# Seven sweeps of block products for the out-projection of a decoder block

## The chip, the cores and the metric

The kernel runs on one core of a Trainium2 chip. The metric is device microseconds of one execution. TensorE multiplies, VectorE and ScalarE work on what it needs and leaves, GpSimd does small copies, and SyncE issues every transfer between the memory of the core and that of the chip.

## The reference

One layer of a decoder on 2,048 tokens with 1,024 features, in float32. `D_LRU` is 1024, `D_SC` 512, `D_FF` 3072.

```python
h = rms_norm(x, norm1_g[l])
z = jnp.einsum('bsd,de->bse', h, w_in[l])               # 1024 -> 3584
lru_x, lru_gate, sc_b, sc_c, sc_x = jnp.split(z, splits, axis=-1)
lru_x = causal_dwconv(lru_x, lru_conv_w[l]) + lru_conv_b[l]
y_lru = rg_lru(lru_x, ...) * jax.nn.gelu(lru_gate)
y_sc = sc_b * causal_dwconv(sc_c * sc_x, sc_conv_w[l])
y_mix = jnp.concatenate([y_lru, y_sc], axis=-1)         # 1536
x = x + jnp.einsum('bse,ed->bsd', y_mix, w_out[l])      # the out-projection
h = rms_norm(x, norm2_g[l])
u = causal_dwconv(jnp.einsum('bsd,df->bsf', h, w_up[l]), ffn_conv_w[l])
gate, up = jnp.split(u, 2, axis=-1)
x = x + jnp.einsum('bsf,fd->bsd', jax.nn.gelu(gate) * up, w_down[l])
...
return rms_norm(x, final_g)
```

## The kernel before

Everything is held with features on the 128 partitions and tokens along the row. The tokens are worked in two halves of 1,024, each of two blocks of 512. The stages follow each other on TensorE: in-projection, recurrence and short convolution of half 0 (here called in0), out-projection of half 0 (out0), in1, out1, then up- and down-projection of both halves (up0, down0, up1, down1).

Each product is made of three matmuls in a rounded format: an operand is split into a rounded part `hi` (a ScalarE copy) and the rest `lo` (a VectorE subtraction) by `split`, and `hi·hi`, `hi·lo` and `lo·hi` are added up in PSUM.

*The order.* TensorE and SyncE run in the order in which the program text issues their instructions. The other engines' instructions are ordered by a planner, by the place in the text, brought forward by `high_priority`: 120 places for whatever empties PSUM, 90 for splits of weights. SyncE issues transfers one after the other, and a transfer whose tile or data isn't ready holds up all behind it.

*The in-projection.* `in_phase` goes through 12 units in the order `UNITS` (L0 L1 S0 L2 L3 S1 L4 L5 S2 L6 L7 S3). A unit of kind L is 128 features of the recurrence (two input products, two gate products, a scan), a unit of kind S 128 features of the short convolution (three input products). `load_weights` loads 512 KB of weights for one product, splits them and calls `tick`. A unit's result `y` (128 × 1,024) is written to the chip's memory by `defer(4, ...)`: four `tick`s later, which is after the fourth weight load behind it. `tick` sends what is due from the head of a list, in order, so an entry that isn't due holds back those behind it. After units 3 to 8 `between` calls `down_sums`, which loads four blocks of `w_down`, makes four sums (S1 to S4) and writes them out, with `defer(3, ...)`.

*The out-projection.* `project` takes a block of 512 tokens at a time and fills eight PSUM banks, one for each 128 of the 1,024 output features. It goes through the 12 rows of 128 features of `y` two at a time: `load_k2` loads 1 MB of `w_out` and two blocks of 256 KB of `y` and splits them. At the end of a block the residual (x) is added from PSUM and the sum is stored, its squares added to an accumulator. During out0 `x1_beside` loads and splits x of half 1, during out1 `h_beside` calls `h_prep` four times, which makes h of half 0 and its combinations for the up-projection.

*The down-projection.* `sweeps` treats its product as 2 × 2 blocks: output features in two halves, input features in pairs of 128, tokens in two blocks. Seven products of sums of blocks take the place of eight products of blocks. `SWEEPS` names the weight block and the data block of each sweep, `TAKEN` the output blocks to which a sweep's PSUM is added (or from which it is subtracted). Four banks `x` run through sweeps 0, 2, 4 and 6 without being cleared; sweeps 1, 3 and 5 have four banks `y` of their own. A step is one load of 512 KB of weights and 512 KB of data, two splits of each and 24 matmuls. The data are written by `up_rest`: blocks B11, B21, B22 and the combinations T1 to T4.

*Buffers.* Raw loads have two tiles (`wr`), split operands 10 pages of 4 KB (`w`), long-lived pages 28 (`act`), short-lived ones 7 (`tmp`); the sums of squares, their splits and roots, `down_sums` and `sq` live in `tmp`.

Of the kernel before, what the change touches and what calls it, by code (L numbers as in the profile page):

```python
# [7 lines left out]
F32 = mybir.dt.float32  # L8
# [20 lines left out]
NI = NFF // 2  # L29
W_OPS = ["W21", "W11", "W22", "W12"]  # L30
# [34 lines left out]
def block_kernel(  # L65
# [34 lines left out]
    y_d = [[dr.tile([P, T], F32, name=f"y_d{h}_{k}") for k in range(NOUT)] for h in range(NH)]  # L100
    f_d = [{o: [dr.tile([P, 2, NB], F32, name=f"f_d{h}_{o}_{k}") for k in range(NI // 2)] for o in F_OPS} for h in range(NH)]
    s_d = {o: [dr.tile([P, 2, NB], F32, name=f"s_d{o}_{k}") for k in range(NI // 2)] for o in S_OPS}
# [72 lines left out]
    def tick():  # L175
        for w in waiting:
            w[0] -= 1
        while waiting and waiting[0][0] <= 0:
            _, dst, src = waiting.pop(0)
            nc.sync.dma_start(dst, src)  # L180
# [209 lines left out]
    def in_phase(half, acts, acc, between):  # L390
# [27 lines left out]
        for n, (kind, c) in enumerate(UNITS):  # L418
# [22 lines left out]
            defer(4, y_d[half][n], y)  # L441
# [4 lines left out]
    def load_k2(src, spilled, t, k, name, ypage):  # L446
        raw = raw_tile(f"wr_{name}_{k}")
        w = raw[:, 0:4, :].rearrange("p (k a) c -> p k (a c)", k=2)
        nc.sync.dma_start(w, src[k : k + 2].rearrange("k p m -> p k m"))
        for i in range(2):  # L450
            nc.sync.dma_start(raw[:, 4 + i, :], spilled[k + i][:, blk(t)])
        tick()
        out = []
        for i in range(2):
            hi = flat(wpage(f"wh_{name}_{k + i}"))
            lo = flat(wpage(f"wl_{name}_{k + i}"))
            yb = ypage(f"yb_{name}_{k + i}")
            with tc.high_priority(offset=HW):
                split(yb[:, 0, :], yb[:, 1, :], raw[:, 4 + i, :])
                split(hi, lo, w[:, i, :])  # L460
            out.append(((hi, lo), yb))
        return out

    def project(half, nk, src, spilled, name, residual, done, beside, late=None, last_k=0):
        step = 0
        for t in range(T // NB):
            pss = [pst(f"{name}{half}_{t}_{i}") for i in range(KC)]
            fin = last_k if t == T // NB - 1 else 0
            held = []
            res = None  # L470

            def steps(k, wt, yb, ms):
                for m in ms:
                    mm3(pss[m], wcol(wt, m), (yb[:, 0, :], yb[:, 1, :]), k == 0, k == nk - 1)

            wts = None
            for k in range(nk):
                if k % 2 == 0:
                    wts = load_k2(src, spilled, t, k, f"{name}{half}_{t}", act if last_k else wpage)
                wt, yb = wts[k % 2]  # L480
                if k == nk - 4:
                    res = [residual(t, i) for i in range(KC // 2)]
                if t > 0 and late is not None and k < 3:
                    if k == 2:
                        late()
                    steps(k, wt, yb, range(KC - 1))
                    held.append((k, wt, yb))
                    if k == 2:
                        for h in held:
                            steps(*h, (KC - 1,))  # L490
                        held = []
                elif k >= nk - fin:
                    held.append((k, wt, yb))
                else:
                    steps(k, wt, yb, range(KC))
                beside(step)
                step += 1
            for i in range(KC // 2):
                for m in (2 * i, 2 * i + 1) if held else ():
                    for h in held:  # L500
                        steps(*h, (m,))
                    with tc.high_priority(offset=HP):
                        nc.vector.tensor_tensor(res[i][:, m % 2, :], pss[m], res[i][:, m % 2, :], ALU.add)
                    done(t, i, res[i], m % 2)
                if not held:
                    with tc.high_priority(offset=HP):
                        for m in range(2):
                            nc.vector.tensor_tensor(res[i][:, m, :], pss[2 * i + m], res[i][:, m, :], ALU.add)
                    done(t, i, res[i], None)
# [14 lines left out]
    def x_residual(half):  # L524
        def get(t, i):
            r = res_page(f"xr{half}_{t}_{i}", i % 2)
            o = half * T + t * NB
            nc.sync.dma_start(r, xT[2 * i : 2 * i + 2, :, o : o + NB].rearrange("m p c -> p m c"))
            return r

        return get

    def x2_residual(half, alloc):
        def get(t, i):
            r = alloc(f"x2r{half}_{t}_{i}")
            nc.sync.dma_start(r, x2_d[half][i][:, :, blk(t)].rearrange("m p c -> p m c"))
            return r

        return get
# [124 lines left out]
    def up_rest(half, j, ug, un):  # L664
        cg, cu = flat(tmp(f"cg{half}_{j}")), flat(tmp(f"cu{half}_{j}"))
        conv(cu, un, 3, O_FCW + 3 * (NFF + j))
        conv(cg, ug, 3, O_FCW + 3 * j)
        nc.scalar.activation(cg, cg, AF.Gelu_apprx_tanh)
        nc.vector.scalar_tensor_tensor(cu, cg, -1.0, cu, ALU.mult, ALU.mult)
        when = {NFF - 2: 3, NFF - 1: 6}.get(j, 1)  # L670
        i = j // 2

        def put(op, src):
            defer(when, f_d[half][op][i // 2][:, i % 2, :], src)

        t0, t1 = blk(0), blk(1)
        if j % 2 == 0:
            put("B11", cu[:, t0])
            even.append(cu)
            return  # L680
        a, b, c, d = even.pop(), cu, cg, flat(tmp(f"tt{half}_{j}"))
        put("B21", b[:, t0])
        put("B22", b[:, t1])
        nc.vector.tensor_tensor(c[:, t0], a[:, t0], a[:, t1], ALU.subtract)
        nc.vector.tensor_tensor(d[:, t0], b[:, t1], a[:, t1], ALU.subtract)
        nc.vector.scalar_tensor_tensor(c[:, t1], c[:, t0], -1.0, b[:, t1], ALU.mult, ALU.subtract)
        nc.vector.scalar_tensor_tensor(d[:, t1], c[:, t1], -1.0, b[:, t0], ALU.mult, ALU.subtract)
        put("T1", c[:, t0])
        put("T2", c[:, t1])
        put("T3", d[:, t0])  # L690
        put("T4", d[:, t1])
# [25 lines left out]
    def down_sums(i):  # L717
        a, b, c = tmp(f"sa{i}"), tmp(f"sb{i}"), tmp(f"sc{i}")
        for o, dst in zip(W_OPS, (a[:, 0, :], a[:, 1, :], b[:, 0, :], b[:, 1, :])):
            nc.sync.dma_start(dst, w_down[W_OPS.index(o), i // 2].rearrange("p (k c) -> p k c", k=2)[:, i % 2, :])  # L720
# [5 lines left out]
        for o, src in zip(S_OPS, (c[:, 0, :], c[:, 1, :], a[:, 0, :], b[:, 1, :])):  # L726
            defer(3, s_d[o][i // 2][:, i % 2, :], src)

    def sums_at(first, i0, also=None):
        def between(n):  # L730
            if also is not None:
                also(n)
            if first <= n < first + NI // 2:
                down_sums(i0 + n - first)

        return between
# [73 lines left out]
    in_phase(0, None, ss1[0], sums_at(3, 0))  # L810
# [5 lines left out]
    def x1_beside(s):  # L816
        if s in (4, 5, 6, 7, 16, 17, 18, 19):
# [4 lines left out]
    def out_done(half):  # L822
        def done(t, i, r, part):
            store_pair(x2_d[half][i], t, r)
            add_squares(ss2[half], t, i, r, f"b{half}")

        return done

    project(0, NOUT, w_out, y_d[0], "o", x_residual(0), out_done(0), x1_beside)
# [13 lines left out]

    in_phase(1, x1, ss1[1], sums_at(3, NI // 2, late_mean(ss2[0], "b0", rs2[0], 1)))

# [10 lines left out]
    project(1, NOUT, w_out, y_d[1], "o", x_residual(1), out_done(1), h_beside(0, (3, 6, 16, 18)))  # L856
# [5 lines left out]
    def down_w(o, i2):  # L862
        if o in W_OPS:
            return w_down[W_OPS.index(o), i2].rearrange("p (k c) -> p k c", k=2)
        return s_d[o][i2]
# [10 lines left out]
    def down0_done(key, m, r):  # L876
        if m % 2 == 0:
            return
        mh, t = PLACE[key]
        store_pair(x3_d[2 * mh + m // 2], t, r, 2 if key == "21" else 4)  # L880
        add_squares(ss3, t, 0 if key in ("11", "22") and m == 1 else 1, r, f"c0{key}{m}")

# [7 lines left out]
        down0_done,  # L890
# [68 lines left out]

def _arrange(i):  # L960
# [8 lines left out]
    for g, name in enumerate(("lru_wa", "lru_wx")):  # L969
# [5 lines left out]
    out["w_out"] = w[[c if kind == "L" else NLRU + c for kind, c in UNITS]]  # L975
    w = f["w_down"][0].reshape(NI // 2, 2, 2, P, 2, NB)
    out["w_down"] = np.stack(
        [w[:, :, kh, :, mh].transpose(0, 2, 1, 3).reshape(NI // 2, P, T) for mh, kh in ((1, 0), (0, 0), (1, 1), (0, 1))]
    )
# [40 lines left out]
```

## Time and profile before

| | |
|---|---|
| median of 3 runs | 2334.21 us (2332.16 to 2335.15) |
| the profiled execution | 2334.49 us |
| its span | 2332.7 us |
| in0 | 0 to 344.1 us |
| out0 | 344.1 to 476.2 us |
| in1 | 476.2 to 804.4 us |
| out1 | 804.4 to 937.1 us |
| up0, down0 | to 1395 and to 1623.5 us |
| up1, down1 and the end | to about 2079 and to 2332.7 us |

In the lines below, PE is TensorE's matmuls and PEld its weight loads, DVE is VectorE, ACT ScalarE, POOL GpSimd, SP SyncE; L189 is line 189 of the kernel. A line of the chain has the start, the duration, and what ran or was waited for; a line of the timeline the start, the duration, the engine and the instruction. In a table by stage each engine has its busy time and, in brackets, its instructions; then come the granted clock, the busy share of the transfer engines and GB/s. In a line of a group the two numbers after the first bar are busy microseconds and mean nanoseconds of one; after the second bar stands the idle time ahead of them.

### The profile page before, as it was taken

Reading aid. Unit: us, or ns where it says so; the run is one execution under the profiler, and the core shown is the slowest. Engines: PE = TensorE matmul, PEld = TensorE weight load, DVE = VectorE, ACT = ScalarE, POOL = GpSimd, SP = SyncE. Lnnn points to the kernel's source line nnn. Section 1 sums busy time; section 2 is a strip of 40 time slices with the busy share of each in tenths; the row PEclk is TensorE's granted clock in tenths of the full one; section 3 lists DMA queues with packets and bytes.
Section 4 is the critical chain, followed back from the end, with each engine's and each line's share of the span. In section 5 each row is a group of like instructions: output and inputs, shape, how many; then the busy total and the mean of one; then the engine's idle time right before and its main releaser. Section 6 shows DMA issues by size and latency. Waiting matters only on the chain.

```text
span 2332.7 us, 26351 instructions
## 1 busy us (share of the span) xinstructions
PE 2306.0 (99%) x10128; PEld 1903.2 (82%) x10128; DVE 1693.3 (73%) x1890; ACT 1125.5 (48%) x1254; POOL 135.7 (6%) x194
## 2 busy tenths in 40 slices
PE   8999999999999999999999999999999999999997
PEld 7888888888888887888888888888888888887885
DVE  7766665666666777888787877678788787886556
ACT  5553454445543644554444444445544444443343
POOL 0000000000000000011111110000011111100000
PEclk9999999999999999999999999999999999999998
DMA  4134335632334366332333337576223232348654
GB/s 151 68 120 138 138 130 189 251 104 68 133 125 158 116 221 223 117 114 99 111 107 109 105 135 280 198 252 235 86 91 113 91 113 93 117 173 318 244 189 180
DMA packets 141183, 349.99 MB, mean 150 GB/s; under 512 B 13056, under 2 KB 16256, under 8 KB 141056
## 3 DMA queue, kind: packets, MB, share of 16 engines
q1 hardware_dynamic: 141056, 348.30, 42.6%
q8 instruction: 79, 1.29, 0.2%
q14 instruction: 48, 0.39, 0.1%
HBM read 258.07 MB, written 90.18 MB: 149 GB/s over the span
## 4 chain that ended last, share of the span: by engine, by line
PE 95%; DVE 3%; DMA 1%; ACT 1%; issue 0%; SPq 0%; DVEq 0%; ACTq 0%
PE zin_b L222 26%; PE zx L608 22%; PE zc L608 11%; PE o L189 11%; PE dx L754 9%; PE dy L754 8%; PE za L608 6%; PE zi_b L222 1%; PE zr_b L222 1%; DMA wr_d<-s_dS 0%; DVE x2r L791 0%; DVE x2r L898 0%; DMA wr_o<-y_d 0%; DMA fx<-x_d 0%; DVE fl_d L184 0%
## 5 line engine op out<-in xcount | busy, mean ns | idle before, releaser
L222 PE MATMUL zin_b<-xh,wh_in 128*128 128x512 f32 x896 | 277.9, 391 | 5.3 <-DVE ss_a L258 2.6
L222 PE MATMUL zin_b<-xl,wh_in 128*128 128x512 f32 x896 | 277.1, 390 | 0.3 <-DVE xl L380 0.3
L222 PE MATMUL zin_b<-xh,wl_in 128*128 128x512 f32 x896 | 276.9, 390 | 0.0
L189 PE MATMUL o<-yb_o,wh_o 128*128 128x512 f32 x768 | 236.8, 389 | 1.3 <-ACT wh_o L183 1.3
L222 PEld LDWEIGHTS zin_b<-xh,wh_in 128*128 128x128 f32 x896 | 169.0, 189 | 41.7 <-DVE ss_a L258 3.5
L222 PEld LDWEIGHTS zin_b<-xl,wh_in 128*128 128x128 f32 x896 | 168.7, 189 | 36.6 <-DVE xl L380 1.8
L222 PEld LDWEIGHTS zin_b<-xh,wl_in 128*128 128x128 f32 x896 | 168.7, 188 | 35.2
L184 DVE TENSOR_TENSOR fl_d<-wr_d,fh_d 128x1024 fp32r<-128x1024 f32 x84 | 102.8, 1223 | 101.2 <-ACT fh_d L183 99.1
L183 ACT ACTIVATE fh_d<-wr_d 128x1024 fp32r<-128x1024 f32 x84 | 89.0, 1060 | 177.7 <-PE dy L754 79.7
L189 PEld LDWEIGHTS o<-yb_o,wh_o 128*128 128x128 f32 x768 | 144.0, 188 | 31.9 <-ACT wh_o L183 2.1
L184 DVE TENSOR_TENSOR wla_up<-wr_up,wha_up 128x1024 fp32r<-128x1024 f32 x48 | 58.8, 1226 | 140.4 <-ACT wha_up L183 140.4
L754 PE MATMUL dx<-fl_d,wh_d 128*128 128x512 f32 x384 | 149.6, 390 | 1.3 <-DVE fl_d L184 1.3
L189 PE MATMUL o<-yb_o,wl_o 128*128 128x512 f32 x384 | 149.7, 390 | 1.1 <-DVE wl_o L184 1.1
L183 ACT ACTIVATE wh_in<-wr_in 128x1024 fp32r<-128x1024 f32 (+1 forms) x62 | 60.2, 975 | 186.3 <-DMA wr_in<-in_w_in 174.7
L754 PE MATMUL dx<-fh_d,wh_d 128*128 128x512 f32 x384 | 149.4, 389 | 0.0
L754 PE MATMUL dx<-fh_d,wl_d 128*128 128x512 f32 x384 | 149.4, 389 | 0.0
L584 DVE TENSOR_TENSOR wr_up<-wr_up 128x512 f32<-128x512 f32 x192 | 130.2, 686 | 9.2 <-DMA wr_up<-in_w_up 7.6
L184 DVE TENSOR_TENSOR wl_d<-wr_d,wh_d 128x1024 fp32r<-128x1024 f32 x84 | 102.6, 1221 | 40.8 <-ACT wh_d L183 38.3
L184 DVE TENSOR_TENSOR wl_in<-wr_in,wh_in 128x1024 fp32r<-128x1024 f32 (+1 forms) x62 | 69.1, 1118 | 83.4 <-ACT wh_in L183 75.3
L608 PE MATMUL zc<-hhB,whd_up 128*128 128x512 f32 x384 | 126.0, 389 | 0.0
L282 DVE SCALAR_TENSOR_TENSOR cu<-un,prm,cu 128x1024 f32<-128x1024 f32 x96 | 122.7, 1278 | 4.3 <-ACT cu L278 4.3
L282 DVE SCALAR_TENSOR_TENSOR cg<-ug,prm,cg 128x1024 f32<-128x1024 f32 x96 | 122.9, 1280 | 0.7
(238 smaller groups left out, 5289.4 us busy)
## 6 DMA issues: line engine op xcount, KB each, us to landing
wr_up<-in_w_up SPq DMA_DIRECT2D x96, 512.0 KB, 4.8
wr_in<-in_w_in SPq DMA_DIRECT2D x54, 512.0 KB, 4.2
wr_o<-in_w_out SPq DMA_DIRECT2D x24, 1024.0 KB, 7.1
wr_d<-s_dS SPq DMA_DIRECT2D x48, 512.0 KB, 3.8
wr_d<-f_d_T SPq DMA_DIRECT2D x48, 512.0 KB, 4.8
f_d_B<-cu SPq DMA_DIRECT2D x72, 256.0 KB, 2.2
wr_d<-in_w_down SPq DMA_DIRECT2D x36, 512.0 KB, 3.7
wr_d<-f_d_B SPq DMA_DIRECT2D x36, 512.0 KB, 4.7
```

What stands on the lines that cost most here:

```text
L183: nc.scalar.activation(r32(hi), src, AF.Copy)
L184: nc.vector.tensor_tensor(r32(lo), src, hi, ALU.subtract)
L189: nc.tensor.matmul(ps, r32(a), r32(b), start=(first and i == 0), stop=(last and i == 2))
L222: nc.tensor.matmul(ps[t], r32(a), r32(b[:, blk(t)]), start=(first and i == 0), stop=(last and i == 2))
L282: nc.vector.scalar_tensor_tensor(dst, src[:, k : k + T], col(o_w + k), dst, ALU.mult, ALU.add)
L584: nc.vector.tensor_tensor(raw[:, o, :], raw[:, a, :], raw[:, b, :], ALU.add)
L608: nc.tensor.matmul(ps, r32(p[:, s]), r32(self.hs[k][x][o]), start=f and i == 0, stop=l and i == 2, skip_group_check=True,)
L754: nc.tensor.matmul(ps[m], r32(p), r32(x[:, k, :]), start=first and i == 0 and n == 0, stop=(last or not on_x) and i == ni - 1 and n == 2, ...
```

## The change

The out-projection is done by `sweeps`, with six pairs of rows of `y` (`NO = 6`) where the down-projection has twelve. `project` and `load_k2` go.

- `w_out` is laid out by the host in the four blocks that `w_down` has.
- After an even unit the block B11 of its `y` is written out; after an odd unit `combine` makes T1 to T4 from the pair (four VectorE instructions of 512 columns, into two `tmp` pages) and six blocks are written. All wait for the fourth `tick`, as `y` did.
- `down_sums` becomes `sums` for both matrices, writes after two `tick`s instead of three, and is called after units 2 to 10: in in0 for six of `w_out` and three of `w_down`, in in1 for the other nine of `w_down`.
- `tick` sends whatever is due, also from behind an entry that isn't.
- x of half 1 is prepared at the even steps 2 to 16 of out0, h of half 0 at steps 2, 6, 10 and 15 of out1 (of 21).
- The residual pages of the out-projection come from `act`, in out1 for two of the four output blocks from other pools.

```diff
+NO = NOUT // 2
...
-        while waiting and waiting[0][0] <= 0:
-            _, dst, src = waiting.pop(0)
+        due = [w for w in waiting if w[0] <= 0]
+        waiting[:] = [w for w in waiting if w[0] > 0]
+        for _, dst, src in due:
             nc.sync.dma_start(dst, src)
...
-            defer(4, y_d[half][n], y)
+            if n % 2 == 0:
+                put(y_d[half], 4, n // 2, "B11", y[:, blk(0)])
+                even = y
+            else:
+                c, d = flat(tmp(f"yc{half}_{n}")), flat(tmp(f"yd{half}_{n}"))
+                combine(y_d[half], 4, n // 2, even, y, c, d)
             between(n)
...
+    def put(dst, when, i, op, src):
+        defer(when, dst[op][i // 2][:, i % 2, :], src)
+
+    def combine(dst, when, i, a, b, c, d):
+        t0, t1 = blk(0), blk(1)
+        nc.vector.tensor_tensor(c[:, t0], a[:, t0], a[:, t1], ALU.subtract)
+        nc.vector.tensor_tensor(d[:, t0], b[:, t1], a[:, t1], ALU.subtract)
+        nc.vector.scalar_tensor_tensor(c[:, t1], c[:, t0], -1.0, b[:, t1], ALU.mult, ALU.subtract)
+        nc.vector.scalar_tensor_tensor(d[:, t1], c[:, t1], -1.0, b[:, t0], ALU.mult, ALU.subtract)
+        for op, src in zip(
+            ("T1", "T2", "B21", "T3", "B22", "T4"), (c[:, t0], c[:, t1], b[:, t0], d[:, t0], b[:, t1], d[:, t1])
+        ):
+            put(dst, when, i, op, src)
...
-    def down_sums(i):
+    def sums(src, dst, i):
...
-            defer(3, s_d[o][i // 2][:, i % 2, :], src)
+            put(dst, 2, i, o, t)
...
-    in_phase(0, None, ss1[0], sums_at(3, 0))
+    in_phase(0, None, ss1[0], sums_at({n: (w_out, so_d, n - 2) if n < 2 + NO else (w_down, sd_d, n - 2 - NO) for n in range(2, 11)}))
...
-        if s in (4, 5, 6, 7, 16, 17, 18, 19):
+        if s % 2 == 0 and 2 <= s <= 2 * KC:
...
-    project(0, NOUT, w_out, y_d[0], "o", x_residual(0), out_done(0), x1_beside)
+    sweeps(
+        0,
+        out_w,
+        y_d[0],
+        NO,
+        "o",
+        x_residual(0, lambda key, n: act(n)),
+        store_done(x2_d[0], ss2[0], "b0"),
+        x1_beside,
+    )
...
-    in_phase(1, x1, ss1[1], sums_at(3, NI // 2, late_mean(ss2[0], "b0", rs2[0], 1)))
+    in_phase(
+        1,
+        x1,
+        ss1[1],
+        sums_at({n: (w_down, sd_d, n + 1) for n in range(2, 11)}, late_mean(ss2[0], "b0", rs2[0], 1)),
+    )
...
-    project(1, NOUT, w_out, y_d[1], "o", x_residual(1), out_done(1), h_beside(0, (3, 6, 16, 18)))
+    def res_alloc(key, n):
+        return res_page(n, 1) if key == "12" else tmp(n) if key == "21" else act(n)
+
+    sweeps(
+        1,
+        out_w,
+        y_d[1],
+        NO,
+        "o",
+        x_residual(1, res_alloc),
+        store_done(x2_d[1], ss2[1], "b1"),
+        h_beside(0, (2, 6, 10, 15)),
+    )
```

More of the change, by code (lines that the diff above doesn't have):

```diff
@@ L440, in in_phase @@
                     cur = lru_conv(nxt[1], half, ps_n, rs)
-            defer(4, y_d[half][n], y)
-            between(n)
[L446 to L509, printed above, removed]
@@ L732, in between @@
                 also(n)
-            if first <= n < first + NI // 2:
-                down_sums(i0 + n - first)
+            if n in at:
+                sums(*at[n])
         return between
@@ L874, in down_residual @@
         return get
[L876 to L881, printed above, removed]
     sweeps(
@@ L974, in _arrange @@
     w = f["w_out"][0].reshape(NOUT, P, D)
[L975 to L979, printed above, removed]
+    out["w_out"] = _blocks(w[[c if kind == "L" else NLRU + c for kind, c in UNITS]], NO)
+    out["w_down"] = _blocks(f["w_down"][0], NI)
     out["w_up"] = f["w_up"][0].reshape(KC, P, 2 * NFF, P).transpose(2, 1, 0, 3).reshape(2 * NFF, P, D)
```

83 lines of the change are left out of this document (40 added, 43 removed).

## The prediction

> **What bounds the kernel now.** I read the page's busy shares first, then the chain that ended last at the borders of the stages, then a table of busy time by stage.
>
> ```profile
> PE 2306.0 (99%) x10128; PEld 1903.2 (82%) x10128; DVE 1693.3 (73%) x1890; ACT 1125.5 (48%) x1254; POOL 135.7 (6%) x194
> ```
> ```profile
> 344.12 63.25 PE o L189 x279
> ...
> 476.18 21.76 PE zin_b L222 x96
> ...
> 804.39 75.95 PE o L189 x335
> ...
> 937.11 2.72 PE zx L608 x12
> ...
> 1492.93 32.64 PE dy L754 x144
> ```
>
> TensorE is the bound: 99% busy, and the chain is almost wholly its matmuls. One matmul takes 32.64/144 = 0.2267 us from start to start. Out0 lasts 476.18 − 344.12 = 132.06 us and out1 937.11 − 804.39 = 132.72 us. The last row, one sweep of down0, is 144 matmuls without a pause.
>
> ```profile
> core 0: us, PE busy (x) PEld busy (x) DVE busy (x) ACT busy (x) POOL busy (x), PEclk, DMA share, GB/s
> 0.00:344.10 344.10, 337.02 (x1467) 277.14 (x1468) 227.51 (x260) 181.41 (x194) 13.67 (x38) 0.99 0.35 121
> 344.10:476.20 132.10, 131.18 (x578) 107.99 (x577) 77.14 (x87) 57.54 (x67) 0.19 (x1) 1.00 0.60 216
> 476.20:804.40 328.20, 328.20 (x1449) 271.76 (x1449) 213.66 (x221) 168.71 (x174) 3.59 (x11) 1.00 0.34 114
> 410.00:432.00 22.00, 21.08 (x92) 16.84 (x91) 16.60 (x21) 12.37 (x15) 0.00 (x0) 1.00 1.00 369
> 804.40:826.00 21.60, 21.60 (x97) 17.86 (x97) 19.77 (x23) 9.70 (x12) 0.00 (x0) 1.00 0.79 282
> 804.40:936.90 132.50, 131.11 (x576) 107.69 (x576) 97.72 (x115) 56.47 (x68) 0.00 (x0) 1.00 0.59 215
> 936.90:1395.00 458.10, 458.10 (x2022) 379.32 (x2022) 375.54 (x437) 230.16 (x273) 56.76 (x95) 1.00 0.33 112
> 1395.00:1623.50 228.50, 228.50 (x1009) 189.18 (x1009) 171.02 (x179) 106.22 (x107) 1.64 (x3) 1.00 0.69 241
> 2105.00:2127.00 22.00, 20.08 (x82) 16.11 (x81) 11.33 (x13) 7.42 (x7) 0.00 (x0) 0.92 0.98 358
> ```
>
> Read here the VectorE column (the third busy time): 97.72 us in out1, 77.14 in out0. The rows 344.10 and 804.40 (132 us each) are the out stages; 0.00 and 476.20 are in0 and in1; the others serve as bounds.
>
> **The change, part by part.**
>
> *Matmuls.* The old loop runs 12 rows × 2 blocks × 8 columns × 3 = 576 per half. Seven sweeps run 7 × 6 × 4 × 3 = 504. That is 144 fewer in both halves, 144 × 0.2267 = −32.6 us. The Trainium skill (TensorE: Matmul & The Clock Gate, section on the 56 ns gap) puts a warm 512-column matmul at 215.7 ns; by that the term would be an estimated 31.1 us. The trace's interval decides.
>
> *The old loop's pauses.* Out0 needs 576 × 0.2267 = 130.56 us, so 1.50 us of it and 2.16 us of out1 are not matmuls at full pace. The loop empties all eight banks at once between its two token blocks; the sweeps have no such border, and the sweep of down0 above has no pause: −3.7 us. Together −36.3.
>
> *VectorE in the out stages.*
>
> ```profile
> L184 DVE TENSOR_TENSOR wl_o<-wr_o,wh_o 128x1024 fp32r<-128x1024 f32 x48 | 58.7, 1223 | 43.5 <-ACT wh_o L183 42.8 <-issue 0.5
> ...
> L184 DVE TENSOR_TENSOR yb_o<-wr_o,yb_o 128x512 fp32r<-128x512 f32 x48 | 32.9, 686 | 33.1 <-ACT yb_o L183 33.1
> ...
> L183 ACT ACTIVATE fh_d<-wr_d 128x1024 fp32r<-128x1024 f32 x84 | 89.0, 1060 | 177.7 <-PE dy L754 79.7 <-PE dx L754 75.4 <-issue 12.7
> ...
> L508 DVE TENSOR_TENSOR xr<-o,xr 128x512 f32<-128x512 f32 x32 | 20.1, 683 | 11.9 <-PE o L189 11.9
> ```
> ```profile
> 817.14 0.69 DVE L557 TENSOR_TENSOR ha<-hb,ha 128x512 f32<-128x512 f32 x1
> 817.75 0.68 DVE L558 SCALAR_TENSOR_TENSOR hq<-hc,hb 128x512 f32<-128x512 f32 x1
> ...
> 835.62 1.22 DVE L184 TENSOR_TENSOR hlB<-ha,hhB 128x1024 fp32r<-128x1024 f32 x1
> 836.75 1.22 DVE L184 TENSOR_TENSOR hlB<-hb,hhB 128x1024 fp32r<-128x1024 f32 x1
> ```
>
> Back to back, an instruction of 1,024 columns costs 1.13 us from start to start, one of 512 costs 0.61. Per half the old loop has 24 of each split and 16 additions: 24 × 1.74 + 16 × 0.61 = 51.5. The new one has 42 splits of 1,024, 32 additions (eight takings × four banks) and the last unit's four combinations: 42 × 1.13 + 36 × 0.61 = 69.4. So +18 us of VectorE work in a stage that shrinks to 504 × 0.2267 = 114.2 us. Out0: 95 of 114 us, 83%, which fits: 0. Out1, with its four preparations of h: 97.7 + 18 = 115.7 of 114.2, which doesn't. It loses at least 1.5 us. At the 92% of the row 804.40 (19.77 of 21.60) it needs 126 us, a loss of 12; at the 82% of the up phase 141 us, a loss of 27. I take 95%, near the 92% row of this very stage: 121.8, a loss of 7.5.
>
> ScalarE gains 42 splits of 1,024 for 48 smaller ones; with 57.5 us busy now it stays near half: 0. PSUM: a sweep on its own banks is emptied by at most eight additions (5 us) while the next sweep runs 16 us: 0.
>
> *The first six steps of an out stage.* A step is now 24 matmuls, 5.44 us. Raw tiles allow a load two to three steps ahead. The last unit's six combination blocks are issued on SyncE after the load of step 3; SyncE waits there for VectorE, and the loads of steps 4 and 5, the 2 MB of residual pages and the next x or h page are queued behind it.
>
> ```profile
> 349.33 1.22 DVE L367 TENSOR_TENSOR sv<-sv,sb 128x1024 f32<-128x1024 f32 x1
> ```
> ```profile
> 812.72 1.22 DVE L367 TENSOR_TENSOR sv<-sv,sb 128x1024 f32<-128x1024 f32 x1
> ```
> ```profile
> 1409.05 0.91 SPq L180 DMA_DIRECT2D f_d_B<-cu  x2
> 1410.00 1.15 SPq L180 DMA_DIRECT2D f_d_T<-cg  x2
> 1411.19 1.45 SPq L180 DMA_DIRECT2D f_d_T<-tt  x2
> ```
> ```profile
> 2101.62 8.52 DMA wr_d<-s_dS
> ```
> ```profile
> wr_in<-in_w_in SPq DMA_DIRECT2D x54, 512.0 KB, 4.2
> ...
> wr_d<-f_d_T SPq DMA_DIRECT2D x48, 512.0 KB, 4.8
> ```
>
> In out0 the last y ends 6.4 us into the stage; four combinations and a split or two between them make it 10, six issues (0.91 + 1.15 + 1.45) 14. The load of step 4 would land 5 us later (4.8 the median), near 19, and with 3.3 us of splits (two ScalarE passes of 1.06, one VectorE pass) be ready at 22.5 against 21.8. Step 5 stands behind step 4's load, 2.1 MB of residual, 0.5 MB of x and its own 1 MB: 4.7 MB at 369 GB/s, 12.8 us, ready near 31 against 27.2. Loss 4 us. In out1 the last y ends 9.5 us into the stage, 3.1 later: loss 7, during which VectorE works off h, so it isn't added to the 7.5 above in full: the two overlap by half, 11 for out1. Bounds: down0 has the same order of spills and residual and kept TensorE busy throughout (228.50 of 228.50: 0); down1 had a load landing after 8.52 us and 82 matmuls in 22 us where 97 fit, 3.4 us lost. With the 8.52 in place of 5, out0 loses up to 8 and out1 up to 15.
>
> The preparations of x and h keep their number and move from 10.9 us steps to 5.4 us ones; the first h pages' loads stand on SyncE ahead of the six spills and wait for a page of the last unit's convolution, which ends before its y: inside the wait already counted, 0.
>
> *The in-projections.* Nine sums instead of six per half and six combinations: 36 × 0.61 = 22 us of VectorE per half in 328, on an engine two thirds busy: 0 by itself. y goes out as 42 blocks of 256 KB instead of 12 of 512 KB, and three more sums move 6 MB: about 11 MB, 33 GB/s beside the present 114 to 121, far from 369: 0. The order on SyncE matters more: a weight load now waits behind six issues that wait for a combination.
>
> ```profile
> 159.65 0.33 SPq L180 DMA_DIRECT2D y_d<-r  x1
> ...
> 162.75 0.58 SPq L201 DMA_DIRECT2D wr_in<-in_w_in  x1
> ```
> ```profile
> 159.16 54.40 PE zin_b L222 x240
> ```
>
> The load at 162.75 feeds the third of the five products that start at 159.16, needed at 180.9. With combinations (4 us with waits) and six issues (3.5) in place of the sums' stores, which now leave two loads earlier, it is issued near 168, lands 4.2 later, at 172, is split by 174.5: 6 us to spare, loss 0. If that cover were gone, each microsecond would be paid at ten units.
>
> *Seven temporary pages in in1.* Two are held by sums of squares, two by the split of the second until its mean; three remain for unit 1's combination pages (two) and unit 2's sums (three).
>
> ```profile
> 569.57 0.91 PE ms_b L253 x4
> 570.47 21.76 PE zin_b L222 x96
> ```
> ```profile
> 574.67 1.22 DVE L260 SCALAR_TENSOR_TENSOR ss_b<-ss_b,ry_b 128x1024 f32<-128x1024 f32 x1
> ```
> ```profile
> 556.38 0.43 SPq L201 DMA_DIRECT2D wr_in<-in_w_in  x1
> ```
>
> The split pages come free at 570.5, the root's page at 575.9. The second combination page waits for one of these, and the load now issued at 556.38 (needed 10.88 us into the block at 570.47, at 581.35) is queued behind its spill: issued at 575 to 579, ready 7 us later: 1 to 5 us late. Loss 2 (0 if pages come free earlier, 6 at most).
>
> *Sum.* −36.3 + 4 + 11 + 2 = −19.3. The profiled execution took 2334.5 us (span 2332.7), 0.3 above the median of 2334.2, so the median should come to **2315**.
>
> **The rivals.**
>
> *All covers hold.* Down0's rows speak for it: same loop, same 0.7 DMA share, no loss. Against it: out1's VectorE sum. 2334.2 − 36.3 + 1.5 = 2299, up to 2306 with small waits.
>
> *VectorE paces out1 at the up phase's 82%.* Loss 27 instead of 11: 2331. Against it: the row 804.40 held 92% with no lost matmul.
>
> *The transfers pace both out stages.* Out0 now moves 216 GB/s × 132.1 us = 28.5 MB; 18.9 of weights and y give way to 22.0, the spill is 1 larger: 32.7 MB, 286 GB/s over 114.2 us. At down0's 241 that lasts 136 us: 21 lost per stage, 2342, slower. It decides where the rate stays under about 262 GB/s. Against it: 358 and 369 in the rows above, the first with loads of this size. The Trainium skill (DMA: Bandwidth & Descriptors, section Bandwidth) says to batch to 1 MiB for 75% of peak, which speaks against replacing 1 MB weight loads by 512 KB ones; one at a time, its fit of 2.0 us plus bytes over 436 GB/s gives an estimated 164 GB/s. The row of 358 GB/s doesn't bear that out for loads in flight together.
>
> *Slower: SyncE's order in the in-projections.* If the combination, last in VectorE's queue behind splits and convolutions, comes 9 us later than I took it, the 6 us of cover are gone and each of ten odd units loses 3: +30, 2345. It turns slower from about 2.4 us per unit.
>
> **How the numbers follow.** Forecast (2306 to 2325) 0.60; covers hold 0.17; VectorE at 82% 0.11; transfers 0.04; SyncE's order 0.06; a gain given back elsewhere, ending level, 0.02. About 0.2% (4.7 us) is what can be told from no change. Faster: 0.60 + 0.17 + 0.07 of the VectorE case = 0.84; same 0.04 + 0.02 = 0.06; slower 0.10. The range 2302 to 2331 leaves out half of "covers hold" (0.08) and the cases above it (0.12).
>
> **What the profile would show.** Out0 near 118 us, out1 near 125, with VectorE at 95% or more there; a gap on TensorE at step 4 or 5 of both stages, released by a load or its split; a gap of some 2 us after ms_b in in1; the other stages unchanged. I am wrong if in0 or in1 grows by more than 5 us, if VectorE has idle time in out1 while TensorE waits, or if the gaps lie at other steps.

## The result and the profile after

The changed kernel takes 2487.03 us (median of 5 runs, 2483.76 to 2490.24) against 2333.58 (5 runs, 2332.16 to 2335.15) for the kernel before: the ratio is 1.0658, 95% interval 1.0643 to 1.0674. The forecast of 2315 and its sign were wrong.

The stages of the profiled executions (2334.49 and 2490.24 us), in us, cut where TensorE starts the next stage's first product:

| kernel | in0 | out0 | in1 | out1 | sum of the four |
|---|---|---|---|---|---|
| before | 344.1 | 132.1 | 328.2 | 132.7 | 937.1 |
| changed, as forecast | 344.1 | 118.3 | 330.2 | 125.2 | 917.8 |
| changed, measured | 425.8 | 119.7 | 419.4 | 126.1 | 1091.0 |

The forecast row comes from its terms: −17.8 and +4 for out0, +2 for in1, −18.5 and +11 for out1. The out stages came within 1.4 us of the forecast; the in-projections, forecast at 2 us more together, lost 81.7 and 91.2. The up- and down-projections hardly moved (1395.6 us before, 1397.4 after).

The table by stage of the changed kernel, columns as before:

```profile
0.00:425.80 425.80, 351.49 (x1467) 285.73 (x1468) 250.38 (x292) 181.87 (x193) 12.03 (x38) 0.90 0.36 120
425.80:545.50 119.70, 116.64 (x505) 95.61 (x505) 94.16 (x101) 63.74 (x63) 3.47 (x4) 0.99 0.79 285
545.50:964.90 419.40, 343.20 (x1449) 279.98 (x1449) 237.84 (x254) 167.51 (x171) 4.71 (x8) 0.89 0.33 111
964.90:1091.00 126.10, 117.88 (x505) 95.51 (x504) 114.49 (x130) 60.81 (x63) 0.40 (x4) 0.97 0.77 276
```

In0 has the same 1,467 matmuls as before, but TensorE is idle 74.3 us of it (425.80 − 351.49) against 7.1 before, and its busy time is 14.5 us longer at a granted clock of 0.90 against 0.99. In1: idle 76.2 against 0.0, busy 15.0 us longer, clock 0.89 against 1.00. No other engine is near full: VectorE is busy 250 of 426 us, the transfer engines 0.36.

TensorE's waits over the whole span, changed kernel (total us, times, longest):

```profile
PE zin_b L228 <- ACT wh_in L189: 93.2, 7, 16.4
PE zin_b L228 <- DVE wl_in L190: 51.4, 9, 7.9
PE oy L692 <- DVE fl_o L190: 6.0, 4, 1.7
PE oy L692 <- ACT fh_o L189: 5.1, 2, 3.5
```

Of the 145 us in the first two rows nothing stood in the profile before: in sixteen waits a product of an in-projection waits for the split of its weights. In the largest of these places the loads are not to blame. First the matmuls around one gap in in0, then SyncE's issues, then the transfers from 115 to 165 us in 40 equal slices:

```profile
135.48 0.61 PE L228 MATMUL zi_b<-xch,gw 128*128 128x512 f32 x2
152.50 1.22 PE L228 MATMUL zin_b<-xh,wh_in 128*128 128x512 f32 x2 [16.40 <-ACT wh_in L189]
153.52 1.05 PE L228 MATMUL zin_b<-xl,wh_in 128*128 128x512 f32 x2
162.44 1.22 PE L228 MATMUL zin_b<-xh,wl_in 128*128 128x512 f32 x2 [7.87 <-DVE wl_in L190]
```
```profile
119.04 0.33 SPq L207 DMA_DIRECT2D wr_in<-in_w_in  x1
...
124.12 0.33 SPq L207 DMA_DIRECT2D wr_in<-in_w_in  x1
...
159.34 1.04 SPq L186 DMA_DIRECT2D so_d_S<-sc  x2
```
```profile
DMA  9700880099500000000000000000000000008946
```

The weights were issued at 119.04 and 124.12 and nothing is in flight from about 129 to 160 us (31 us): they lie in the raw tiles while TensorE stands for 24 us. What they wait for is the order on ScalarE and VectorE. The same unit in the two kernels, VectorE's timeline; first before, where three splits (`wl_in`) stand ahead of the unit's result (`r<-g,r`):

```profile
128.28 1.23 DVE L184 TENSOR_TENSOR wl_in<-wr_in,wh_in 128x1024 fp32r<-128x1024 f32 x1 [5.53 <-ACT wh_in L183]
...
134.27 1.23 DVE L184 TENSOR_TENSOR wl_in<-wr_in,wh_in 128x1024 fp32r<-128x1024 f32 x1
...
140.25 1.23 DVE L184 TENSOR_TENSOR wl_in<-wr_in,wh_in 128x1024 fp32r<-128x1024 f32 x1 [0.91 <-ACT wh_in L183]
...
158.35 1.23 DVE L338 TENSOR_TENSOR r<-g,r 128x1024 f32<-128x1024 f32 x1 [0.35 <-POOL h_last L336]
```

and after, where the splits come behind the result, the combination and the sums of `w_out`:

```profile
155.44 1.23 DVE L344 TENSOR_TENSOR r<-g,r 128x1024 f32<-128x1024 f32 x1 [0.35 <-POOL h_last L342]
156.69 0.69 DVE L463 TENSOR_TENSOR yd<-r,sv 128x512 f32<-128x512 f32 x1
...
158.63 0.69 DVE L660 TENSOR_TENSOR sc<-sa,sb 128x512 f32<-128x512 f32 x1
...
160.56 0.68 DVE L663 TENSOR_TENSOR sb<-sc,sb 128x512 f32<-128x512 f32 x1
161.17 2.35 DVE L190 TENSOR_TENSOR wl_in<-wr_in,wh_in 128x1024 fp32r<-128x1024 f32 x2
```

VectorE executes in the planner's order, so its half of the split comes only after the whole chain of the recurrence has ended (the 7.87 us). ScalarE's half, `wh_in`, stands behind ScalarE's last piece of that chain and starts at 151.41 (the 16.40 us).

Seven gaps hold 140 of the 145 us, and six of them are such pairs of waits. The seventh, 9.6 us in in1, is another thing: a load that is late. SyncE's loads for the sums (L658) wait for the products of the mean (`ms_b`), which hold pages, and the weights are issued behind them. The chain of the changed kernel there:

```profile
638.86 0.69 PE ms_b L259 x3
639.56 0.12 SPq L658
...
641.15 7.04 DMA wr_in<-in_w_in
...
648.21 1.06 ACT wh_in L189
...
649.32 5.74 PE zin_b L228 x18
```

### The profile page after: what moved, and what is told of

It reads as the page before. It is cut to its first block, busy times and chain, and to the rows that moved or that the text cites. A ratio compares the mean times of both kernels' runs of the same rounds, so it can differ in the third digit from the quotient of the medians.

```text
span 2488.4 us, 26274 instructions
## 1 busy us (share of the span) xinstructions
PE 2308.5 (93%) x9984; PEld 1896.5 (76%) x9984; DVE 1773.9 (71%) x1982; ACT 1136.4 (46%) x1242; POOL 137.6 (6%) x194
## 4 chain that ended last, share of the span: by engine, by line
PE 81%; DVE 7%; ACT 3%; DMA 2%; issue 1%; SPq 0%; DVEq 0%; POOL 0%; ACTq 0%; POOLq 0%
PE zx L562 21%; PE zin_b L228 21%; PE zc L562 10%; PE dx L692 8%; PE dy L692 8%; PE za L562 5%; PE ox L692 4%; PE oy L692 2%; DVE r L340 1%; PE zr_b L228 1%; DVE fl_o L190 1%; PE zi_b L228 1%; DVE cv L288 0%; DVE xr L729 0%; DMA x<-in_xT 0%
## 5 line engine op out<-in xcount | busy, mean ns | idle before, releaser
L228 PE MATMUL zin_b<-xh,wh_in 128*128 128x512 f32 x896 | 289.0, 404 | 97.7 <-ACT wh_in L189 93.2
L228 PE MATMUL zin_b<-xh,wl_in 128*128 128x512 f32 x896 | 286.0, 401 | 51.4 <-DVE wl_in L190 51.4
L228 PE MATMUL zin_b<-xl,wh_in 128*128 128x512 f32 x896 | 285.6, 401 | 0.0
L228 PEld LDWEIGHTS zin_b<-xh,wh_in 128*128 128x128 f32 x896 | 174.7, 196 | 138.7 <-ACT wh_in L189 96.2
L228 PEld LDWEIGHTS zin_b<-xl,wh_in 128*128 128x128 f32 x896 | 175.0, 195 | 37.9 <-DVE xl L386 0.3
L562 PE MATMUL zx<-ht,whc_up 128*128 128x512 f32 x384 | 118.2, 389 | 0.0
L692 PE MATMUL dy<-fl_d,wh_d 128*128 128x512 f32 x288 | 113.4, 394 | 2.9 <-DVE fl_d L190 2.9
L189 ACT ACTIVATE wh_d<-wr_d 128x1024 fp32r<-128x1024 f32 x84 | 88.5, 1054 | 59.7 <-DMA wr_d<-sd_d_S 36.2
L573 ACT ACTIVATE ug<-zx 128x512 f32<-128x512 f32 x96 | 57.6, 600 | 126.3 <-PE zx L562 126.3
```

What stands on the lines that cost most here:

```text
L189: nc.scalar.activation(r32(hi), src, AF.Copy)
L228: nc.tensor.matmul(ps[t], r32(a), r32(b[:, blk(t)]), start=(first and i == 0), stop=(last and i == 2))
L562: nc.tensor.matmul(ps, r32(p[:, s]), r32(self.hs[k][x][o]), start=f and i == 0, stop=l and i == 2, skip_group_check=True,)
L573: nc.scalar.activation(dst, self.x, AF.Copy)
L692: nc.tensor.matmul(ps[m], r32(p), r32(x[:, k, :]), start=first and i == 0 and n == 0, stop=(last or not on_x) and i == ni - 1 and n == 2, ...
```

## The experiments

Three theories. PAGES: the planner hands out the short-lived pages of one name in the order of the text. The second combination page (`yd`) needs the odd unit's result, and stands in the text ahead of the pages of `sums`; the loads of the sums stand in SyncE's fixed order ahead of the next weights. So the planner takes these weights to arrive after the result, and orders their splits behind it. SPILLS: the six blocks that are written out behind each odd unit, and their waits on SyncE, delay the weights. WORK: VectorE's added instructions do.

Medians in us, with the ratio to the kernel before measured beside it (2334.60 for E1 to E4, 2334.46 for E5 to E8, 2334.47 for E9 to E12):

| run | edit | median | ratio, 95% interval |
|---|---|---|---|
| E1 | both pages from the long-lived pool | 2359.11 | 1.0105 [1.0088, 1.0122] |
| E2 | only the first of the two | 2486.51 | 1.0654 [1.0638, 1.0670] |
| E3 | kernel before + one short-lived page | 2438.72 | 1.0447 [1.0432, 1.0463] |
| E4 | kernel before + one long-lived page | 2355.78 | 1.0094 [1.0079, 1.0110] |
| E5 | combination one unit later in the text | 2327.71 | 0.9973 [0.9963, 0.9983] |
| E6 | combination in the unit's own dead pages | 2332.45 | 0.9988 [0.9979, 0.9997] |
| E7 | E1 + gate weights' page from another pool | 2330.34 | 0.9986 [0.9977, 0.9995] |
| E8 | sums ahead of the combination in the text | 2349.50 | 1.0066 [1.0052, 1.0080] |
| E9 | E5 + last unit's spills spread | 2323.08 | 0.9955 [0.9943, 0.9968] |
| E10 | E5 + mean one unit later in in1 | 2330.41 | 0.9983 [0.9974, 0.9991] |
| E11 | E5 with three h preparations in out1 | 2327.77 | 0.9975 [0.9964, 0.9985] |
| E12 | E9 and E10 together | 2325.72 | 0.9963 [0.9949, 0.9977] |

**E1, the pages of the combination from the long-lived pool.**

```diff
-                c, d = flat(tmp(f"yc{half}_{n}")), flat(tmp(f"yd{half}_{n}"))
+                c, d = flat(act(f"yc{half}_{n}")), flat(act(f"yd{half}_{n}"))
```

> The changed kernel with both combination pages taken from the long-lived pool (28 pages) instead of the short-lived one (7). Theory PAGES (short-lived pages are given out in the order of the text; the second combination page stands ahead of the pages of the sums, whose loads stand ahead of the next weight loads in SyncE's fixed order; so the planner believes that the weights come after y, and puts their splits behind the chain of y on ScalarE and VectorE, which work in order): in0 falls from 426 to about 345 us, in1 from 419 to about 330, out0 and out1 stay near 120 and 126, the whole about 2487 - 81 - 89 = 2317. Theory SPILLS (six block spills per odd unit wait on SyncE ahead of the weight loads): the spills, their number and SyncE's order are unchanged, so it stays near 2487. Theory WORK (VectorE has too much to do in the in-projections): the work is unchanged, near 2487.

2359.11, where 2317 was expected: 128 us come back with the same instructions, transfers and place in the text. What stayed is mainly another wait, in TensorE's waits of E1:

```profile
PE zr_b L228 <- DVE gw L190: 20.2, 4, 5.2
PE zr_b L228 <- ACT gw L189: 5.4, 3, 2.1
```

The gate weights (`gw`) of the next unit live in the long-lived pool, and their page stands in the text behind `yd`, which now is in that pool. VectorE's timeline of E1 shows their split amid the combination, behind its third instruction:

```profile
163.09 0.68 DVE L464 SCALAR_TENSOR_TENSOR yc<-yc,r 128x512 f32<-128x512 f32 x1
163.69 0.42 DVE L190 TENSOR_TENSOR gw<-wr_in,gw 128x256 fp32r<-128x256 f32 x1
164.02 0.68 DVE L465 SCALAR_TENSOR_TENSOR yd<-yc,r 128x512 f32<-128x512 f32 x1
```

**E2, only the first of the two pages.**

```diff
-                c, d = flat(tmp(f"yc{half}_{n}")), flat(tmp(f"yd{half}_{n}"))
+                c, d = flat(act(f"yc{half}_{n}")), flat(tmp(f"yd{half}_{n}"))
```

> As e1, but only the first combination page (yc) comes from the long-lived pool; the second (yd), which needs the odd unit's y before it can be asked for, stays in the short-lived one. PAGES as a matter of order (which page is asked for first): nothing gained, 2487 within 10. PAGES as a matter of number (seven are simply too few): one page less in demand, a good part of the 170 us gone, 2350 to 2420. SPILLS and WORK: 2487.

2486.51, half a microsecond below the changed kernel. One page fewer in the small pool is worth nothing; the page that waits for the odd unit is what counts.

**E3 and E4, the kernel before with one page more.** One subtraction of 512 columns for each odd unit, into a page that nobody reads, ahead of the sums; no spill, no combination. E4 has `act` in place of `tmp`.

```diff
+            if n % 2 == 1:
+                extra = flat(tmp(f"ye{half}_{n}"))
+                nc.vector.tensor_tensor(extra[:, blk(0)], y[:, blk(0)], y[:, blk(1)], ALU.subtract)
```

> The kernel before, out-projection as it was, with one VectorE subtraction of 512 columns after every odd unit, into a short-lived page that nobody reads, in the text ahead of the sums. 12 instructions in all. PAGES: the splits go behind the chain of y at the units 3, 5 and 7 (three places of the changed kernel's four to five per half): about 100 to 140 us slower than before, 2435 to 2475. SPILLS: no spill is added, 12 x 0.61 = 7 us on an engine two thirds busy: 2334. WORK: 2334.

> As e3, with the page taken from the long-lived pool: the same 12 instructions at the same place. PAGES, SPILLS and WORK all: 2334 within 5. If it is slow like e3, it is the instruction and not the page.

E3: 2438.72, +104 us for twelve subtractions of 0.69 us. TensorE's waits in E3 are of the changed kernel's kind, nine in place of sixteen:

```profile
PE zin_b L222 <- ACT wh_in L183: 67.2, 5, 22.7
PE zin_b L222 <- DVE wl_in L184: 21.4, 4, 6.7
```

E4: 2355.78, +21, more than expected, through the gate weights again (11.6 us in 4 waits on `gw`). With E1 and E2 this settles the cause: a page, its pool and its place. SPILLS and WORK cannot make E3. What the planner reckons is not on record; that it takes the weights to arrive late is the reading that foretold these runs. On the chip the page itself held nothing up in the gap shown (the sums made at 158.63 had been loaded from 111.46 on); only the order was late.

**E5, the combination later in the text.** The pages stay short-lived; the combination of a pair is emitted behind the next unit's sums (the last one behind its own), and its blocks then wait for two `tick`s instead of four.

```diff
+        pair = []
...
-                c, d = flat(tmp(f"yc{half}_{n}")), flat(tmp(f"yd{half}_{n}"))
-                combine(y_d[half], 4, n // 2, even, y, c, d)
+                pair.append((n, even, y))
             between(n)
+            for m, a, b in pair[:]:
+                if n > m or n == len(UNITS) - 1:
+                    pair.remove((m, a, b))
+                    c, d = flat(tmp(f"yc{half}_{m}")), flat(tmp(f"yd{half}_{m}"))
+                    combine(y_d[half], 2 if n > m else 4, m // 2, a, b, c, d)
```

> Changed kernel, but the combination of an odd unit's y stands in the text behind the NEXT unit's products and sums (the last unit's behind its own sums, as now); the two pages stay short-lived ones, all twelve subtractions per unit pair, spills and sums stay. PAGES (the second combination page holds the later pages, and so the weight splits on ScalarE and VectorE, behind the chain of y): the splits are 2 to 5 products ahead again, both in-projections fall back to about 344 and 328 us, and the kernel takes the change's own out-stage gain: 2487 - 82 - 91 = 2314 (2308 to 2325). The gate weights' page, which accounts for the rest in the first experiment (PAGES' second pool), stands where it stood in the kernel before. SPILLS and WORK (the spills in SyncE's order, or the added VectorE work itself, cost the remaining 42 us that the first experiment left): 2340 to 2359.

2327.71, 159 us below the changed kernel and faster than the kernel before. The table by stage of E5:

```profile
0.00:343.50 343.50, 337.82 (x1467) 277.75 (x1468) 242.10 (x287) 182.11 (x192) 12.34 (x37) 0.99 0.43 147
343.50:467.40 123.90, 118.82 (x506) 96.62 (x505) 98.04 (x105) 64.27 (x63) 8.96 (x5) 0.97 0.78 279
467.40:804.10 336.70, 330.48 (x1450) 272.71 (x1449) 233.01 (x252) 169.42 (x173) 10.91 (x8) 0.99 0.41 138
804.10:928.80 124.70, 117.46 (x505) 95.36 (x504) 114.47 (x131) 60.60 (x62) 0.40 (x4) 0.99 0.77 280
```

In0 is back (343.5 against 344.1 before, with all the added work in it), the clock too. It missed the expected 2314 by 14 us: in1 is 8.5 longer than before, and out0 4.2 longer than in the changed kernel, where, as I read it and did not test, the longer in0 had left the engines time.

**E6, E7, E8, three other ways out of the same order.** E6 writes the combination into two pages of the unit that are dead by then (`spare`) and takes none. E7 is E1 with the gate weights' page from the pool of the weights. E8 moves one line, the call for the sums, ahead of the combination. The lines that matter of each:

```diff
E6  +                c, d = spare
E7  -        gw = flat(act(f"gw{half}_{c}"))
E7  +        gw = flat(wpage(f"gw{half}_{c}"))
E8  +            between(n)
```

> Changed kernel, but the combination takes no page at all: it is written into two pages of the unit itself that nobody reads any more. Text order, work, spills and sums unchanged. PAGES: no new page, no new order, so 2314 as for the later combination (2308 to 2325), with the gate weights' split where it was. If it is the place in the text and not the page that orders the splits, this stays near 2487. SPILLS, WORK: 2340 to 2359.

> First experiment's kernel (combination pages from the long-lived pages), and the gate weights' page taken from the pages of the weights instead of the long-lived ones, so that it no longer stands behind the second combination page. PAGES: the waits on gw (20 + 5 us on TensorE in the first experiment) go, and with them most of its 42 us: 2314 to 2325, the upper end if one weight page less in flight costs something. SPILLS, WORK: 2359 stays.

> Changed kernel with one line moved: the sums of w_out stand in the text ahead of the combination of the same unit. Same pages, same instructions. PAGES: the sums' pages are no longer behind the second combination page, but the next unit's are; the splits are 2 to 4 products ahead at every unit instead of 0 to 3, so most of the gaps close: 2330 (2314 to 2380). If the number of pages or the work is what costs, 2487.

E6 gives 2332.45: nothing moved in the text, no page taken, 155 us gone. E7 gives 2330.34: the waits on `gw` are gone (29 us less than E1), though its in0 is 350.5 us, with one wait of 4.4 us for `g`. E8 gives 2349.50, 138 us less by the order of two lines; 27.1 us of waits on `wh_in` stay. All three confirm PAGES in its main part. E8 lies in the range expected of it; E6 and E7 fall short of 2314.

**E9, the last unit's spills spread.** `combine` of the last unit gives each of its six blocks a load count of its own.

```diff
-                combine(y_d[half], 2 if n > m else 4, m // 2, a, b, c, d)
+                combine(y_d[half], 2 if n > m else dict(T1=4, T2=7, B21=8, T3=10, B22=12, T4=14), m // 2, a, b, c, d)
...
-            put(dst, when, i, op, src)
+            put(dst, when[op] if isinstance(when, dict) else when, i, op, src)
```

> The later combination's kernel (2327.7), with one change: the last unit's six combination blocks are no longer issued by SyncE together, but at load counts 4, 7, 8, 10, 12 and 14, each ahead of the step that reads it. SPILL BLOCK (the prediction's term for the first six steps: four subtractions and six spills stand in SyncE's queue ahead of x's load and the weights of steps 4 to 6): out0 goes from 123.9 to about 119 and out1 gains little, so 2323 (2320 to 2326). VECTORE (out0's excess over the matmuls is VectorE's own work, with no wait that the spills make): 2327 to 2328.

2323.08 (2322.55 to 2324.61) against E5's 2327.71 (2326.31 to 2329.14): 4.6 us, for blocks that the edit spreads in out1 as well as in out0. E12 against E10, the same edit on another base, gives 4.7. The chain of E5 in out0 shows the block and x's load, with the residual's SyncE issues between them, ahead of a gap of TensorE:

```profile
354.51 5.59 DMA y_d_T<-yc
...
362.26 9.49 DMA x<-in_xT
...
377.71 7.10 PE oy L697 x23
```

In E9 x's load starts at 361.48 and TensorE goes on at 376.70, only a microsecond earlier; out0 is 122.0 us in E9's profile against 123.9, 118.2 in E12's against 121.9 in E10's. The profiled executions of E5 and E9 lie only 1.7 us apart. So the gain is shown, its seat in the stages only in part.

**E10, the mean one unit later.** In1 of E5 has a gap behind `ms_b`, 6.2 us in two waits, where the prediction had put 2 us. No transfer stands in the chain of E5 there:

```profile
560.90 0.69 PE ms_b L259 x3
...
568.41 1.15 DVE wl_in L190
...
569.60 2.50 PE zin_b L228 x5
```

```diff
-        sums_at({n: (w_down, sd_d, n + 1) for n in range(2, 11)}, late_mean(ss2[0], "b0", rs2[0], 1)),
+        sums_at({n: (w_down, sd_d, n + 1) for n in range(2, 11)}, late_mean(ss2[0], "b0", rs2[0], 2)),
```

> The later combination's kernel (2327.7), with the mean of the second norm (ms_b) formed one unit later in the in-projection of the second half; the same work. PAGES: what holds the weights' split behind ms_b there is again a short-lived page (two of the split of the sum of squares are held until the mean, and unit 2's sums need three); with the mean behind unit 2 the splits of products 10 and 3 stand 23 and 20 VectorE instructions ahead of it instead of 6 and 8 behind: in1 goes from 336.7 to 328 to 330, so 2320 (2318 to 2324). If the 8 us are the mean's own chain and not the order of the splits, 2327 to 2328.

2330.41, no gain. E5's two waits (3.2 and 3.0 us) are gone, but one of 8.5 us stands behind the mean at its new place. TensorE's waits of E10, then its timeline, then ScalarE's:

```profile
PE zin_b L228 <- ACT wh_in L189: 8.5, 1, 8.5
```
```profile
583.82 0.61 PE L259 MATMUL ms_b<-rl_b,ones_r 128*128 128x512 f32 x2
592.98 1.22 PE L228 MATMUL zin_b<-xh,wh_in 128*128 128x512 f32 x2 [8.54 <-ACT wh_in L189]
```
```profile
584.51 1.27 ACT L263 ACTIVATE ry_b<-ms_b,eps 128x512 f32<-128x512 f32 x2
...
590.71 1.27 ACT L329 ACTIVATE i<-zi_b,prm 128x512 f32<-128x512 f32 x2
591.85 1.07 ACT L189 ACTIVATE wh_in<-wr_in 128x1024 fp32r<-128x1024 f32 x1
```

ScalarE makes the split behind the root of the mean (`ry_b`) and the gates of L2 (`i`). The weights had long landed: no transfer is in flight from about 576 to 592 us here, and from 547 to 572 in E5, where ScalarE stands idle for 17.6 us until `ms_b` has come. So the waits behind the mean are again the order of the splits, and the wait followed the mean when it was moved. In1 is 339.7 instead of 336.7. Which page holds the splits there is not settled.

**E11, three preparations of h in out1 instead of four.** The fourth block of h is left out and the up-projection reads the first in its place, so this kernel does not compute the layer; it serves to take work off VectorE.

```diff
-                hs[half].append(h_prep(half, len(hs[half]), rs2[half][0]))
+                hs[half].append(hs[half][0] if half == 0 and len(hs[half]) == 3 else h_prep(half, len(hs[half]), rs2[half][0]))
```

> The later combination's kernel (2327.7), with one of the four normalised blocks of x2 that VectorE and ScalarE make inside out1 left out (the up-projection reads the first block in its place): some 9.5 us of VectorE work less in out1, TensorE's work unchanged. VECTORE (the prediction's term: out1 is paced by VectorE): out1 goes from 124.7 to 117 to 120, so 2321 (2318 to 2324). SPILL BLOCK or loads pace out1: 2326 to 2328.

2327.77 against E5's 2327.71. VectorE loses 7.9 us of work in out1 (106.56 against 114.47), and out1 does not shrink (127.9 against 124.7). But the work that was taken out lay where TensorE waits for nothing. Out1 in the two profiles, in us, cut where TensorE goes on after its last gap:

| kernel | stretch | length | TensorE idle | VectorE busy |
|---|---|---|---|---|
| E5 | 804.1 to 872.7 | 68.6 | 7.2 | 65.07 |
| E5 | 872.7 to 928.8 | 56.1 | 0.05 | 49.41 |
| E11 | 805.2 to 876.4 | 71.2 | 9.2 | 64.88 |
| E11 | 876.4 to 933.1 | 56.7 | 0.1 | 41.68 |

In the first stretch, which holds all the gaps, VectorE has the same work in both kernels and is busy 95% of the time in E5. So E11 shows that VectorE's work behind the last gap costs nothing. It does not test for the first 68 us that VectorE paces out1, the prediction's term. The chain of E11 there goes through many VectorE instructions and through four loads into the two raw tiles, each followed by the splits that free the tile; two of the loads:

```profile
831.92 7.07 DMA wr_o<-y_d_T
...
865.44 5.70 DMA wr_o<-in_w_out
```

Whether VectorE or the turnaround of the raw tiles sets the first half of out1 was not tried, and stays open.

**E12, E9 and E10 together.**

> Spills spread and the mean one unit later together, on the later combination; all of the reference is computed. If the two are separate waits, their gains add: 2327.7 - 5 - 7 = 2316 (2312 to 2322), which is the prediction's own sum for the change (2315). If the time won in one is given back in the next stage, 2320 to 2324.

2325.72, above the 2312 to 2322 expected: E9's edit gains 4.7 us on E10, and E10's gains nothing. E9 alone is the best version and beats both kernels: 11 us (0.9955) under the kernel before, 164 under the changed one, with all the change's work in it.

## Why the prediction was wrong

*Matmuls, −32.6, and the old loop's pauses, −3.7:* the matmuls went as counted (505 in each out stage, borders included, where 578 and 576 stood); the pauses were not measured by themselves. Out0 and out1 measure 119.7 and 126.1 us where 118.3 and 125.2 were forecast. For out0 that is in part luck: with the in-projection in order it takes 123.9 (E5).

*Slower in the in-projections: the step that failed.* "Seven temporary pages in in1" saw that pages of one pool would be short there, and priced it at 2 us (0 to 6) through SyncE: a page is late, so a load is issued late. That happened in one gap, the seventh above, and cost 9.6 us. "The in-projections" took 0, with 6 us of cover for a weight load behind six spills. Both asked when the load is issued. Neither asked where the load's split stands on ScalarE and VectorE, which run in a planned order, and six of the seven long gaps lie there; the front part of this document says so of the planner, and the prediction made no use of it. The page made the planner order the splits behind a result that, in the gap shown, ended 20 us after TensorE had come to the weights (156.7 against 136.1), in both halves. The term measures 81.7 us in in0 and 91.2 in in1 where 0 and 2 stood. Where that order is undone (E5), in0 costs 0 as forecast, SyncE's queue included.

*The rival of the other sign* had the right place (the next product's weights, once per odd unit) and the wrong mechanism, SyncE's order; by it 2345. The early-warning sentence held: wrong "if in0 or in1 grows by more than 5 us".

*The gap behind ms_b, 2 us, 6 at most:* in the changed kernel it is 9.6 us, and the mechanism is the one forecast: the load of the weights is issued at 641.15, behind loads that wait for pages held until `ms_b`. It was mis-sized. In E5 the gap is 6.2 us and no load is late; there it is the order of the splits.

*The spill block, 4 in out0:* right in the main. TensorE's only idle time in out0 of the changed kernel is 1.7 and 1.4 us, 27 to 31 us into the stage, which is step 5. Spreading the blocks of both halves gained 4.6 and 4.7 us of the whole (E9, E12).

*VectorE in out1, 7.5 at 95%, with half of the spill block's 7:* the size of the stage came out (124.7 to 126.1 against 125.2), the mechanism is open. VectorE is busy 91% of the stage (114.49 of 126.10), and 92% up to the last gap. TensorE's gaps lie at steps 3 and 4 (1.7 and 1.5 us) and, 64 to 70 us into the stage, where none was forecast (3.5 and 1.5). What sets them is not settled, because E11 took its work out behind them. So the right size is no evidence for the term.

*Transfers pace the out stages:* no. They ran at 285 and 276 GB/s, above the 262 from which it would have decided, and out0 of E12 took 118.2 us. The fit that the prediction set beside this rival, 2.0 us plus bytes over 436 GB/s, stands in the Trainium skill (DMA: Bandwidth & Descriptors, section "Anatomy of one DMA — SWDGE (gpsimd) path") for transfers that GpSimd issues; those here are SyncE's, and no run tests it.

*The sum.* With the splits in order (E5) the profiled four stages come to 928.8 us: 11.0 above the forecast's 917.8, of which in1 is 6.5, out0 5.6, in0 and out1 together −1.1. E5's one edit took back 159 of the 172 us between 2487 and 2315.

## What to carry to other kernels

Where a planner orders the in-order engines, a new buffer is a new place in every later order: before adding a page, follow what stands behind it in the same pool, what loads stand behind those in the fixed queue, and where the planner will then put their splits. A wait on a split whose load landed long ago (here 31 us with no transfer in flight) is a wait on order, not on bandwidth, and it can be undone by moving one line or taking a dead page. And a cover of 6 us named for one queue says nothing of the other queues that the same data pass.

## What the hardware showed that was not expected

The growth in TensorE's idle time explains 143.4 of the 172.9 us that the in-projections lost; the other 29.5 are slower matmuls. Behind the 7.87 us wait at 162.44, TensorE's timeline of the changed kernel:

```profile
163.46 1.05 PE L228 MATMUL zin_b<-xh,wh_in 128*128 128x512 f32 x2
164.31 1.05 PE L228 MATMUL zin_b<-xl,wh_in 128*128 128x512 f32 x2
...
167.69 0.62 PE L228 MATMUL zin_b<-xh,wl_in 128*128 128x512 f32 x2
168.15 0.63 PE L228 MATMUL zin_b<-xh,wh_in 128*128 128x512 f32 x2
```

Two matmuls take 0.85 us from start to start (163.46 to 164.31) for the first 5 us, then 0.46: half speed, some 2.5 us lost behind this gap. The granted clock is 0.50 from 140.3 to 167.6 us and 1.00 behind it. The Trainium skill (TensorE: Matmul & The Clock Gate, Part 1, sections "What's actually happening" and "Wait — 56ns, not 53.3ns?") has the clock fall to half after an idle window of about 3.4 us and return after a busy one of that length, in windows that run on whatever the kernel does, with 426.7 ns from start to start for a cold matmul of 512 columns. The trace agrees on the interval (0.425 us); the slow stretch lasts 5.2 us here (162.44 to 167.69). It does not agree on the idle window: behind a wait of only 1.98 us (`wl_in` at 224.26) the granted clock is 0.51 from 225.6 to 229.1 us, and here the trace decides. The prediction priced waits by their length alone; a wait of some microseconds costs more than that.
